# Eight experts on one core: x of four experts in one load, larger VectorE transposes, and evictions moved to ScalarE

## The chip, the cores and the metric

The kernel runs on one core of a Trainium2 chip. The metric is the device time of one execution in microseconds, as the median of several runs. Beside these runs there is one profiled execution, from which all views of the trace come.

## The reference

Eight experts each take their own 256 tokens through a two-layer network; nothing is routed.

```
x [8, 256, 512]   w1 [8, 512, 2048]   w2 [8, 2048, 512]   b1 [8, 2048]   b2 [8, 512]     all float32
h   = relu(x @ w1 + b1)        per expert: 256x512 times 512x2048
out = h @ w2 + b2              per expert: 256x2048 times 2048x512, float32
```

## The kernel before

**Stages.** For each expert e there are a load of `w1` (4 MB in DRAM), a load of `w2` (4 MB), transposes of x, a first product and a second product. The main loop has eleven steps s: it runs `first_product(s)` and, three steps behind (`LAG = 3`), `second_product(s - 3)`. Everything is computed in fp16 with fp32 accumulation; the DMAs that GpSimd issues cast fp32 to fp16 on the way, those that SyncE and ScalarE issue do not.

**Loads and their order.** All weight loads are issued by GpSimd, one after the other in an order written out by hand (the list `ring`), and they go through one software DMA queue. `w1` has three buffers, `w2` three. So the loads of w1 for experts 0, 1 and 2 are issued at once (`load_w1`, L84); the load of w1 for expert 3 has to wait until `first_product(0)` has read the first buffer, and what stands behind it in GpSimd's order (w2 of expert 0, x of experts 4 to 7) waits with it. The x of experts 0 and 1 comes as two SyncE loads of 512 KB (L190), 4 KB to a partition, in fp32, and VectorE casts each (L201). The x of experts 2 and 3 is one casting GpSimd load, that of experts 4 to 7 another (`load_x`, L76).

**Row order.** Where one load takes several experts, a partition holds several consecutive token rows, and the rows of one expert lie in P / n partitions. `transposes` turns x[token, hidden] into xT[hidden, token] by VectorE's 32x32 block transposes: L109 where an expert was loaded by itself (32x256 elements an instruction), L112 where two or four came together (32x256 and 32x512). They restore the plain column order with a strided write. ScalarE's relu with bias (L128) then writes `hT` in the order that the grouped stores want.

**First product.** 16 column blocks j of four matmuls (L121) into one of three PSUM tiles `ph`, each evicted by one relu on ScalarE, which needs the transposed bias `b1T` (VectorE, L208). In the middle of the loop (j = 8) the transposes of the next expert are emitted.

**Second product and stores.** For each half tb of the tokens a matmul with b2 (L171) and 16 matmuls (L178) into `po`. `store` evicts po[0] on VectorE (L156) and po[1] on ScalarE (L157); experts 0 to 3 are evicted in 4 pieces of 32 partitions a half, experts 4 and 5 in 2 pieces of 64, experts 6 and 7 in one. The results of experts 0 to 3 and of 4 and 5 are stored as two groups by GpSimd (`flush`, L140) after the last weight load; experts 6 and 7 are stored by SyncE and ScalarE (L164).

The instruction order within VectorE and ScalarE is set by a scheduler at build time, except for what `ordered` pins: the matmuls and GpSimd's DMAs.

Of the kernel before, what the change touches and what calls it, by code (L numbers as in the profile page):

```python
# [10 lines left out]
def kernel(  # L11
# [37 lines left out]
    w2_pool = ctx.enter_context(tc.tile_pool(name="w2", bufs=3))  # L49
    x_pool = ctx.enter_context(tc.tile_pool(name="xp", bufs=1))  # L50
# [18 lines left out]
    results = {}  # L69
    group_of = {first + i: (first, n) for first, n in GROUPS.items() for i in range(n)}  # L70

    def load_x(first, n):

        R = n * T // P
        t = x_pool.tile([P, R, H], fp16, tag=f"x{first}", name=f"x{first}")
        ordered(nc.gpsimd.dma_start(  # L76
            out=t, in_=x[first : first + n].rearrange("e (p r) h -> (e p) r h", r=R)
        ))
# [9 lines left out]
    def load_w2(e):  # L88
# [3 lines left out]
        for lo in range(0, nJ, half):  # L92
            ordered(nc.gpsimd.dma_start(out=w2_sb[e][:, lo : lo + half], in_=src[:, lo : lo + half]))  # L93

    def transposes(e):


        t, p0, R = x16[e]
        n = R // nTB
        xT[e] = xT_pool.tile([P, nKC, T], fp16, tag="xT", name="xT")  # L100
        for g in range(T // R // B):
            src = t[p0 + B * g : p0 + B * (g + 1)]
            for b in range(nB):
                block = src[:, :, b * (H // nB) : (b + 1) * (H // nB)].rearrange(
                    "p (n tb) (i kc) -> p tb kc n i", tb=nTB, kc=nKC)
                out = xT[e][b * B : (b + 1) * B].rearrange(
                    "p kc (tb g i n) -> p tb g kc n i", tb=nTB, i=B, n=n)
                if n == 1:
                    nc.vector.transpose(out=out[:, :, g, :, 0, :], in_=block[:, :, :, 0, :])  # L109
                    continue  # L110
                for tb in range(nTB):
                    nc.vector.transpose(out=out[:, tb, g], in_=block[:, tb])  # L112

    def first_product(e):
        hT[e] = hT_pool.tile([P, nJ, T], fp16, tag="hT", name="hT")
        split = group_of[e][1] if e in group_of else 1
        for j in range(nJ):
            bias_at = j * B + e * nB + nB - 1
            ph = psum_h.tile([P, T], fp32, tag="ph", name="ph")
            for kc in range(nKC):  # L120
                ordered(nc.tensor.matmul(  # L121
                    out=ph,
                    lhsT=w1_sb[e][:, kc, :].rearrange("p (q j) -> p q j", j=nJ)[:, :, j],
                    rhs=xT[e][:, kc, :],
                    start=(kc == 0),
                    stop=(kc == nKC - 1),
                ))
            nc.scalar.activation(  # L128
                out=hT[e][:, j, :].rearrange("p (tb k i) -> p tb k i", tb=nTB, k=split),
                in_=ph.rearrange("p (tb i k) -> p tb k i", tb=nTB, k=split),  # L130
                func=mybir.ActivationFunctionType.Relu,
                bias=b1T[:, bias_at : bias_at + 1],
                scale=1.0,
            )
            if j == nJ // 2 and e + 1 < E:
                transposes(e + 1)
# [5 lines left out]
    def store(e, po):  # L142
# [10 lines left out]
        at = (e - first) * rows  # L153
        for k in range(split):
            part = slice(k * rows, (k + 1) * rows)
            nc.vector.tensor_copy(out=out_sb[at : at + rows, k * nTB, :], in_=po[0][part])  # L156
            nc.scalar.copy(out=out_sb[at : at + rows, k * nTB + 1, :], in_=po[1][part])  # L157
        dst = out[first : first + n].rearrange("e (p r) h -> (e p) r h", r=split * nTB)
        if e in group_of:
            if e == first + n - 1:  # L160
# [23 lines left out]
                    ))  # L184
        store(e, po)

    x32 = []
    for e in range(nXF32):
        x32.append(out_pool.tile([P, nTB, H], fp32, tag="out", name="x32"))
        nc.sync.dma_start(out=x32[e], in_=x[e].rearrange("(p tb) h -> p tb h", tb=nTB))  # L190
    load_w1(0)
    ordered(nc.gpsimd.dma_start(  # L192
        out=b2_sb,
        in_=b2.rearrange("e h -> (e h)").rearrange("(o f) -> o f", o=1),
    ))
    ordered(nc.gpsimd.dma_start(out=b1_rows, in_=b1.rearrange("e (b i) -> (e b) i", b=nB)))  # L196
    nc.vector.memset(ones1, 1.0)  # L197

    for e in range(nXF32):
        t = x_pool.tile([P, nTB, H], fp16, tag=f"x{e}", name=f"x{e}")  # L200
        nc.vector.tensor_copy(out=t, in_=x32[e])  # L201
        x16[e] = (t, 0, nTB)
        if e == 0:
            transposes(e)


    for b in range(nB):
        nc.vector.transpose(  # L208
# [57 lines left out]
```

## Time and profile before

| | |
|---|---|
| median of 3 runs | 181.56 us (181.4 to 181.62) |
| span of the profiled execution | 179.8 us |
| median less span | 1.8 us, outside the profiled span |
| TensorE matmul busy | 129.0 us (72%) |
| VectorE busy | 87.8 us (49%) |
| ScalarE busy | 70.2 us (39%) |
| DMA | busy share 9 or more tenths in 38 of 40 slices |
| HBM read, written | 71.39 MB, 4.19 MB |

In the profile PE is TensorE's matmul, PEld its weight load, DVE is VectorE, ACT is ScalarE, POOL is GpSimd and SP is SyncE. The trailing q on an engine's name means its sequencer, which issues DMAs and handles semaphores. `x32` in the code is the fp32 staging tile of x; the trace names the loaded and the cast tile both `x`.

### The profile page before, as it was taken

What the parts mean: (1) busy time and instruction counts of PE and PEld (TensorE: products, weight loads), DVE (VectorE), ACT (ScalarE), POOL (GpSimd) and SP (SyncE); (2) the same over time, 40 slices, a digit from 0 to 9 for tenths busy, and PEclk for the clock granted to TensorE, in tenths of its full rate; (3) what the DMA queues carried; (4) which work ended last, traced back from release to release, by engine and by line L of the source; (5) the groups of instructions that cost most, each with busy time, mean ns of one, the idle gap of its engine ahead of it and who ended that gap; (6) DMA issues with size and microseconds to landing.
All of it is one profiled execution on the core that took longest, in us unless ns stands there. A gap on an engine that the chain in (4) does not pass through costs nothing.

```text
span 179.8 us, 1957 instructions
## 1 busy us (share of the span) xinstructions
PE 129.0 (72%) x784; PEld 86.2 (48%) x784; DVE 87.8 (49%) x125; ACT 70.2 (39%) x151; POOL 13.4 (7%) x28
## 2 busy tenths in 40 slices
PE   0005199959995930999869597969788887999740
PEld 0004089948993410794369244943387433343310
DVE  1999933985000199999999998000600020301010
ACT  0000569947993050482189005940298020111010
POOL 7000003020201010001000001000100020020000
PEclk9999999987999995599999799996999999999995
DMA  5999999999999999999999999999999999999995
GB/s 215 252 230 195 233 208 201 233 228 200 215 231 193 219 230 222 197 226 230 208 204 230 219 200 226 230 211 200 230 219 201 226 211 208 217 211 221 324 456 215
DMA packets 3828, 40.56 MB, mean 226 GB/s; under 512 B 460, under 2 KB 476, under 8 KB 1132
## 3 DMA queue, kind: packets, MB, share of 16 engines
q0 software_dynamic: 3232, 38.35, 96.5%
q1 hardware_dynamic: 476, 1.70, 2.4%
q10 hardware_dynamic: 112, 0.39, 0.5%
q8 instruction: 6, 0.10, 0.2%
q14 instruction: 2, 0.02, 0.0%
HBM read 71.39 MB, written 4.19 MB: 420 GB/s over the span
## 4 chain that ended last, share of the span: by engine, by line
DMA 55%; PE 32%; ACT 3%; another core or an unknown queue 3%; POOL 2%; issue 1%; POOLq 0%; ACTq 0%
DMA w1sb<-in_w_dram 43%; PE po L178 16%; PE ph L121 15%; DMA w2sb<-in_w_dram 12%; ACT out L157 3%; PE po L171 1%; POOL w1sb L84 1%; ACT hT L128 1%; POOL w2sb L93 0%; POOL x L76 0%; POOL b_sb L192 0%; POOL b_rows L196 0%; POOLq L250 0%; ACTq L128 0%
## 5 line engine op out<-in xcount | busy, mean ns | idle before, releaser
L121 PE MATMUL ph<-xT,w1sb 128*128 128x256 f16 x512 | 64.9, 293 | 34.1 <-DMA w1sb<-in_w_dram 21.5
L121 PEld LDWEIGHTS <-w1sb 128*128 128x128 f16 x512 | 59.8, 147 | 40.1 <-DMA w1sb<-in_w_dram 31.8
L178 PE MATMUL po<-w2sb,hT 128*128 128x512 f16 x256 | 60.0, 394 | 9.8 <-DMA w2sb<-in_w_dram 9.8
L112 DVE STREAM_TRANSPOSE xT<-x 32x256 f16<-32x256 f16 (+1 forms) x64 | 53.0, 888 | 26.0 <-DMA x<-in_x_dram 19.2
L128 ACT ACTIVATE hT<-ph,b1T 128x256 f16<-128x256 f32 x128 | 56.2, 474 | 14.4 <-PE ph L121 14.2
L178 PEld LDWEIGHTS <-hT 128*128 128x128 f16 x256 | 25.5, 101 | 44.1 <-issue 17.8
L156 DVE COPY out<-po 32x512 f32<-32x512 f32 (+2 forms) x22 | 15.1, 688 | 53.7 <-PE po L178 53.5
L157 ACT COPY out<-po 32x512 f32<-32x512 f32 (+2 forms) x22 | 12.7, 579 | 68.8 <-PE po L178 68.6
L109 DVE STREAM_TRANSPOSE xT<-x 32x256 f16<-32x256 f16 x32 | 14.0, 436 | 0.5
L93 POOL DMA_DIRECT2D w2sb<-in_w_dram x10 | 5.3, 534 | 71.6 <-PE po L178 71.6
L84 POOL DMA_DIRECT2D w1sb<-in_w_dram x8 | 4.8, 601 | 64.1 <-PE ph L121 63.3
L128 ACT ACT_TABLE_LOAD x1 | 1.3, 1283 | 20.1 <-DVE b1T L208 20.1
L171 PE MATMUL po<-b_sb,ones 1*128 1x512 f16 x16 | 4.8, 379 | 0.0
L208 DVE STREAM_TRANSPOSE b1T<-b_rows 32x512 f32<-32x512 f32 x4 | 4.1, 1031 | 0.1
L201 DVE CAST x<-x 128x1024 f16<-128x1024 f32 x2 | 1.4, 694 | 3.1 <-DMA x<-in_x_dram 3.1
L171 PEld LDWEIGHTS <-ones 1*128 1x128 f16 x16 | 0.9, 92 | 2.1 <-issue 2.1
L140 POOL DMA_DIRECT2D out_dram<-out x2 | 1.1, 538 | 9.8 <-ACT out L157 9.8
L76 POOL DMA_DIRECT2D x<-in_x_dram x2 | 1.1, 552 | 0.0
L197 DVE MEMSET ones<- 1x128 f16 x1 | 0.2, 165 | 0.8 <-PEq L250 0.8
L196 POOL DMA_DIRECT2D b_rows<-in_b_dram x1 | 0.5, 515 | 0.0
L192 POOL DMA_DIRECT2D b_sb<-in_b_dram x1 | 0.5, 513 | 0.0
L250 POOL MEMSET const-float32-0.0<- 128x1 f32 x1 | 0.1, 99 | 0.2 <-issue 0.2
(3 smaller groups left out, 0.3 us busy)
## 6 DMA issues: line engine op xcount, KB each, us to landing
w1sb<-in_w_dram POOLq DMA_DIRECT2D x8, 2048.0 KB, 34.8
w2sb<-in_w_dram POOLq DMA_DIRECT2D x6, 2048.0 KB, 47.2
w2sb<-in_w_dram POOLq DMA_DIRECT2D x4, 1024.0 KB, 23.2
out_dram<-out POOLq DMA_DIRECT2D x1, 2048.0 KB, 19.0
x<-in_x_dram SPq DMA_DIRECT2D x2, 512.0 KB, 3.7
x<-in_x_dram POOLq DMA_DIRECT2D x1, 1024.0 KB, 31.2
out_dram<-out POOLq DMA_DIRECT2D x1, 1024.0 KB, 14.9
x<-in_x_dram POOLq DMA_DIRECT2D x1, 512.0 KB, 24.0
```

The costliest lines, as they stand in the source:

```text
L84: ordered(nc.gpsimd.dma_start(out=w1_sb[e], in_=w1[e].rearrange("(p kc) m -> p kc m", kc=nKC)))
L93: ordered(nc.gpsimd.dma_start(out=w2_sb[e][:, lo : lo + half], in_=src[:, lo : lo + half]))
L109: nc.vector.transpose(out=out[:, :, g, :, 0, :], in_=block[:, :, :, 0, :])
L112: nc.vector.transpose(out=out[:, tb, g], in_=block[:, tb])
L121: ordered(nc.tensor.matmul(out=ph, lhsT=w1_sb[e][:, kc, :].rearrange("p (q j) -> p q j", j=nJ)[:, :, j], rhs=xT[e][:, kc, :], start=(kc == 0),
L128: nc.scalar.activation(out=hT[e][:, j, :].rearrange("p (tb k i) -> p tb k i", tb=nTB, k=split), in_=ph.rearrange("p (tb i k) -> p tb k i", ...
L156: nc.vector.tensor_copy(out=out_sb[at : at + rows, k * nTB, :], in_=po[0][part])
L157: nc.scalar.copy(out=out_sb[at : at + rows, k * nTB + 1, :], in_=po[1][part])
L171: ordered(nc.tensor.matmul(out=t, lhsT=ones1, rhs=b2_sb[0:1, e * H : (e + 1) * H], start=True, stop=False,))
L178: ordered(nc.tensor.matmul(out=po[tb], lhsT=hT[e][:, j, tb * P : (tb + 1) * P], rhs=w2_sb[e][:, j, :], start=False, stop=(j == nJ - 1),))
L201: nc.vector.tensor_copy(out=t, in_=x32[e])
L208: nc.vector.transpose(out=b1T[b * B : (b + 1) * B, nB - 1 - b : nB - 1 - b + nJ * B], in_=b1_rows.rearrange("r (i j) -> r j i", j=nJ),)
```

## The change

- The x of experts 0 to 3 comes in one SyncE load of 2 MB with 16 KB to a partition, into a tile that takes one of the three `w2` buffers; one VectorE cast of 128x4096 elements follows. The GpSimd load of x for experts 2 and 3 is gone; that for experts 4 to 7 stays.
- A partition now always holds 8 rows of one expert (32 partitions to an expert). `transposes` issues 4 instructions of 32x1024 elements for an expert, or, for experts 4 and 5, 8 of 32x512. The output columns are left in the row order of the load; only experts 6 and 7 get their order put right, by the relu's access pattern.
- `store` evicts both halves of experts 0 to 5 on ScalarE; for experts 6 and 7 it stays as it was.
- The memset of `ones1` moves from VectorE to GpSimd.

```diff
-    nXF32 = 2
-    X_LOADS = {2: 2, 4: 4}
+    XG = P // B
+    R = XG * T // P
+    ON_VECTOR = HALVED
...
-    def load_x(first, n):
-        R = n * T // P
+    def rows_of(first):
+        return x[first : first + XG].rearrange("e (p r) h -> (e p) r h", r=R)
+
+    def x_tile(first):
         t = x_pool.tile([P, R, H], fp16, tag=f"x{first}", name=f"x{first}")
...
-        for i in range(n):
-            x16[first + i] = (t, i * (P // n), R)
+        for i in range(XG):
+            x16[first + i] = t[i * B : (i + 1) * B]
+        return t
+
+    def load_x(first):
+        ordered(nc.gpsimd.dma_start(out=x_tile(first), in_=rows_of(first)))
...
+        s = 2 if split_of(e) == 2 else 1
         xT[e] = xT_pool.tile([P, nKC, T], fp16, tag="xT", name="xT")
+        for b in range(nB):
+            src = x16[e][:, :, b * (H // nB) : (b + 1) * (H // nB)].rearrange(
+                "p (s r) (i kc) -> p s kc r i", s=s, kc=nKC)
+            out = xT[e][b * B : (b + 1) * B].rearrange("p kc (r i s) -> p s kc r i", i=B, s=s)
+            for k in range(s):
+                nc.vector.transpose(out=out[:, k], in_=src[:, k])
...
+            columns = ph
+            hidden = hT[e][:, j, :]
+            if split_of(e) == 1:
+                columns = ph.rearrange("p (n tb i) -> p tb i n", tb=nTB, i=B)
+                hidden = hidden.rearrange("p (tb i n) -> p tb i n", tb=nTB, i=B)
             nc.scalar.activation(
-                out=hT[e][:, j, :].rearrange("p (tb k i) -> p tb k i", tb=nTB, k=split),
-                in_=ph.rearrange("p (tb i k) -> p tb k i", tb=nTB, k=split),
+                out=hidden,
+                in_=columns,
...
-            nc.vector.tensor_copy(out=out_sb[at : at + rows, k * nTB, :], in_=po[0][part])
-            nc.scalar.copy(out=out_sb[at : at + rows, k * nTB + 1, :], in_=po[1][part])
+            for tb in range(nTB):
+                to = out_sb[at : at + rows, tb * split + k, :]
+                if tb == 0 and e in ON_VECTOR:
+                    nc.vector.tensor_copy(out=to, in_=po[tb][part])
+                else:
+                    nc.scalar.copy(out=to, in_=po[tb][part])
...
-    x32 = []
-    for e in range(nXF32):
-        x32.append(out_pool.tile([P, nTB, H], fp32, tag="out", name="x32"))
-        nc.sync.dma_start(out=x32[e], in_=x[e].rearrange("(p tb) h -> p tb h", tb=nTB))
+    x32 = w2_pool.tile([P, R, H], fp32, tag="w2", name="x32")
+    nc.sync.dma_start(out=x32, in_=rows_of(0))
     load_w1(0)
...
-    nc.vector.memset(ones1, 1.0)
-
-    for e in range(nXF32):
-        t = x_pool.tile([P, nTB, H], fp16, tag=f"x{e}", name=f"x{e}")
-        nc.vector.tensor_copy(out=t, in_=x32[e])
-        x16[e] = (t, 0, nTB)
-        if e == 0:
-            transposes(e)
+    nc.gpsimd.memset(ones1, 1.0)
+
+    nc.vector.tensor_copy(out=x_tile(0), in_=x32)
+    transposes(0)
...
-            if s in X_LOADS:
-                ring.append((s - 2, load_x, (s, X_LOADS[s])))
+            if s % XG == 0:
+                ring.append((s - 2, load_x, (s,)))
```

More of the change, by code (lines that the diff above doesn't have):

```diff
@@ L70 @@
     group_of = {first + i: (first, n) for first, n in GROUPS.items() for i in range(n)}
-    def load_x(first, n):
-        R = n * T // P
+    def rows_of(first):
+        return x[first : first + XG].rearrange("e (p r) h -> (e p) r h", r=R)
+    def x_tile(first):
         t = x_pool.tile([P, R, H], fp16, tag=f"x{first}", name=f"x{first}")
-        ordered(nc.gpsimd.dma_start(
-            out=t, in_=x[first : first + n].rearrange("e (p r) h -> (e p) r h", r=R)
-        ))
-        for i in range(n):
-            x16[first + i] = (t, i * (P // n), R)
+        for i in range(XG):
[3 more added lines that the diff above has]
+        ordered(nc.gpsimd.dma_start(out=x_tile(first), in_=rows_of(first)))
     def load_w1(e):
@@ L93, in load_w2, with split_of @@
             ordered(nc.gpsimd.dma_start(out=w2_sb[e][:, lo : lo + half], in_=src[:, lo : lo + half]))
+    def split_of(e):
+        return group_of[e][1] if e in group_of else 1
     def transposes(e):
-        t, p0, R = x16[e]
-        n = R // nTB
+        s = 2 if split_of(e) == 2 else 1
         xT[e] = xT_pool.tile([P, nKC, T], fp16, tag="xT", name="xT")
[L101 to L112, printed above, removed]
+        for b in range(nB):
[4 more added lines that the diff above has]
+                nc.vector.transpose(out=out[:, k], in_=src[:, k])
     def first_product(e):
         hT[e] = hT_pool.tile([P, nJ, T], fp16, tag="hT", name="hT")
-        split = group_of[e][1] if e in group_of else 1
         for j in range(nJ):
```

## The prediction

> **What bounds the kernel now.** I read the page's slices and queues first, because a kernel that reads 71 MB in 180 us is likely to be held by its loads.
>
> ```profile
> span 179.8 us, 1957 instructions
> PE   0005199959995930999869597969788887999740
> DVE  1999933985000199999999998000600020301010
> DMA  5999999999999999999999999999999999999995
> GB/s 215 252 230 195 233 208 201 233 228 200 215 231 193 219 230 222 197 226 230 208 204 230 219 200 226 230 211 200 230 219 201 226 211 208 217 211 221 324 456 215
> q0 software_dynamic: 3232, 38.35, 96.5%
> q1 hardware_dynamic: 476, 1.70, 2.4%
> HBM read 71.39 MB, written 4.19 MB: 420 GB/s over the span
> ```
>
> The DMA row is full in every slice but the first and the last, while PE has holes of whole slices. GB/s counts bytes as they are written, so a casting load shows at half of what it reads. The two HBM figures add to 75.6 MB. So the end is set by how soon the DMA engines start, by their rate, and by whether they ever run dry. Next I asked how far ahead of need each load is issued: the timeline of GpSimd and SyncE, and the issue-to-landing time of single loads. First the timeline:
>
> ```profile
> 0.74 0.87 SPq L190 DMA_DIRECT2D x<-in_x_dram  x2
> 1.25 0.67 POOL L84 DMA_DIRECT2D w1sb<-in_w_dram  x1 [0.80 <-POOLq L250]
> 4.00 0.91 POOL L84 DMA_DIRECT2D w1sb<-in_w_dram  x1
> 29.93 0.53 POOL L84 DMA_DIRECT2D w1sb<-in_w_dram  x1 [25.03 <-PE ph L121]
> 30.45 0.54 POOL L93 DMA_DIRECT2D w2sb<-in_w_dram  x1
> 109.72 2.34 ACT L157 COPY out<-po 32x512 f32<-32x512 f32 x4 [10.61 <-PE po L178]
> 147.22 1.06 POOL L93 DMA_DIRECT2D w2sb<-in_w_dram  x2 [16.62 <-PE po L178]
> 158.11 1.07 POOL L140 DMA_DIRECT2D out_dram<-out  x2 [9.83 <-ACT out L157]
> 164.81 0.38 ACTq L164 DMA_DIRECT2D out_dram<-out  x1
> ```
>
> Then, from the view of a line, the landing times of the loads issued at 1.25, 4.00, 29.93 and 30.45 (w1 of experts 0, 2 and 3, w2 of expert 0) and of the two at 147.22 (w2 of expert 7), in this order:
>
> ```profile
> DMA to landing us min/median/max: 14.0/14.0/14.0
> DMA to landing us min/median/max: 34.6/34.6/34.6
> DMA to landing us min/median/max: 17.7/17.7/17.7
> DMA to landing us min/median/max: 26.8/26.8/26.8
> DMA to landing us min/median/max: 16.9/19.3/21.6
> ```
>
> w1 of expert 3 lands at 29.9 + 17.7 = 47.6 and the w2 behind it at 30.5 + 26.8 = 57.3: one 4 MB load takes 9.7 us of the DMA engines, 433 GB/s read. The last weights were issued at 147.2 and landed up to 21.6 us later, though the two halves need only 9.7: there the queue is some 12 us ahead. At one place it is thinner. All that GpSimd could issue at the start is landed at 4.0 + 34.6 = 38.6, and the next load waits until 29.93 for PE to finish the first product of expert 0. Its transfer fills 37.9 to 47.6, so it had 8.0 us in hand, less the time from issue to the first byte. That time is at most about 3.4 us (next fence: the software queue moves nothing before 4.6, issued at 1.25) and at least about 1 us (SyncE issues at 0.74, and the first slice of the window from 1.5 with data starts at 1.73). **So the first product of expert 0 may end about 4.6 to 7 us later than now, at 34.5 to 37, before the DMA engines run dry.** This is the number on which the sign hangs.
>
> **The load of x.** The bytes in 40 slices and the queues of the window from 1.5 to 4.6 us, and the queue of weights in that from 4.6 to 14.2:
>
> ```profile
> GB/s 0 0 0 211 0 0 0 0 264 159 476 317 529 317 529 317 476 370 476 370 423 370 476 370 370 476 317 476 317 529 317 529 317 529 317 529 264 581 264 581
> q1 hardware_dynamic: 265, 1.02, 85.3%
> q0 software_dynamic: 128, 2.10, 102.9%
> ```
>
> Until 4.6 only SyncE's 1 MB moves (hardware queue), then w1 of expert 0. The removed load of experts 2 and 3 lies in the software queue between w1 of experts 1 and 2. The same 2 MB of DRAM are read either way, only 1 MB of it earlier: w1 of expert 0 comes 2.4 us later (1.05 MB at 433 GB/s) and w1 of expert 2 when it did before. In rate, 1.02 MB took about 2.9 us in the first window (1.73 to 4.6), 0.4 of it ramp, so 2.5 against 2.42 at the weights' rate: rows of 16 KB can gain some 0.1 us on each MB that used to come in other rows, 0.0 to 0.25 us in all. I take 0.15 us gained.
>
> **The chain to the first product's end**, which must fit into those 4.6 to 7 us. Its rows:
>
> ```profile
> 4.09 0.69 DVE L201 CAST x<-x 128x1024 f16<-128x1024 f32 x1 [3.10 <-DMA x<-in_x_dram]
> 4.82 7.18 DVE L109 STREAM_TRANSPOSE xT<-x 32x256 f16<-32x256 f16 x16
> 12.76 3.13 DVE L109 STREAM_TRANSPOSE xT<-x 32x256 f16<-32x256 f16 x7
> 15.90 4.17 DVE L208 STREAM_TRANSPOSE b1T<-b_rows 32x512 f32<-32x512 f32 x4
> 20.14 1.28 ACT L128 ACT_TABLE_LOAD   x1 [20.14 <-DVE b1T L208]
> b_rows<-in_b_dram POOLq DMA_DIRECT2D x1, 64.0 KB, 13.2
> L112 DVE STREAM_TRANSPOSE xT<-x 32x512 f16<-32x512 f16 x32 | 40.3, 1331 | 19.8 <-DMA x<-in_x_dram 19.2 <-PE ph L121 0.3
> L109 DVE STREAM_TRANSPOSE xT<-x 32x256 f16<-32x256 f16 x32 | 14.0, 436 | 0.5
> L112 DVE STREAM_TRANSPOSE xT<-x 32x256 f16<-32x256 f16 x32 | 12.7, 444 | 6.2 <-PE ph L121 6.0
> ```
>
> 1. Landing: 512 KB were ready for VectorE at 4.09. Another 1.57 MB at 412 to 433 GB/s (the rates of the last paragraph) add 3.6 to 3.8: 7.8.
> 2. Cast: 4 times the elements, at most 4 x 0.694 = 2.8; a fixed part that is paid once lowers it. I take 2.6: 10.4.
> 3. Transposes of expert 0: no row has 32x1024. Per element the rows give 436/256 = 1.70 ns (one expert a load), 1.73 (two) and 1331/512 = 2.60 (four). The instruction's length isn't what makes the dear row dear, I think, but its write: with n experts a load the inner output step is n elements, 1, 2 and 4. The new code writes expert 0 with inner step 1, like L109. So 4 x 1024 x 1.70 = 7.0, a little less for fewer starts: 6.9, with 10.6 (at 2.60) as the dear end and 6.4 as the cheap one. End: 17.3.
> 4. Bias: `b1_rows` landed at 2.41 + 13.2 = 15.6 behind w1 of expert 0, and now comes 2.4 later, 18.0. VectorE may by then be in a transpose of expert 1 (1.7 long; now the scheduler puts 7 of 16 ahead of the bias). I take 18.9; 4.17 of work: 23.1.
> 5. From the bias's end (20.07) to the first product's end (29.93) it took 9.86 us, with the table load and 52 matmuls in it. Unchanged: 32.9.
>
> That is 3.0 us later than now, inside the 4.6 to 7. No hole, and nothing later is late: the second product that frees w2's first reused buffer is the same (x takes one of three buffers, read out by 10.4, so the fourth w2 load still waits for the second product of expert 0).
>
> **The other parts** are off the path. Evictions: 20 of 22 VectorE copies go to ScalarE, where one takes 2.34/4 = 0.585 us, 11.7 us more of ScalarE's 179.8. If they run in loop order, 7 instead of 4 stand between PE's end of a second product and the next relu, 1.75 us for each of experts 0 to 3, 0.6 for 4 and 5; if the scheduler puts the first half's four ahead, nothing. The relus and so PE's next first product wait behind them. The cover is the queue's lead, 12 us at the last weight load, 11 at the grouped stores, issued at 158.11 behind weights that land at 147.7 + 21.6 = 169.3; without it each would count in full. VectorE's transposes for experts 4 to 7 fall from 32 x 1.331 = 42.6 to about 4 x 7 = 28 us, which helps nobody while DMA is full. ScalarE's relus keep their element count; their new access pattern could cost or save a little of 0.47 us each, under the same cover. The memset on GpSimd is 0.1 us, before or behind issues that are ahead. The last store starts when the DMA engines have worked off what is queued, so it moves with the sum.
>
> **The sum:** 179.8 - 0.15 = 179.65 of span, and with the 1.8 us outside it (181.56 - 179.8) 181.4 us. A measurement of this kernel can tell about 0.2%, 0.36 us, from no change, so this is "the same".
>
> **The rivals.** *A: the weight queue runs dry once, at about 36 us, because x comes late (slower).* SyncE's load and w1 of expert 0 may share the engines. For it, a window with both kinds of queue busy (168.6 to 170.6):
>
> ```profile
> q0 software_dynamic: 68, 0.52, 62.0%
> q10 hardware_dynamic: 63, 0.26, 31.4%
> q1 hardware_dynamic: 21, 0.08, 9.5%
> ```
>
> 68 packets of one against 84 of the others: they alternate. Against it, the row of 164.9 to 168.2:
>
> ```profile
> q0 software_dynamic: 104, 0.77, 105.5%
> ```
>
> The stores issued at 164.81 got nothing for over 3 us: what an engine already has goes first, and at the start SyncE's rows are there first. If they alternate from 4.6 on, 16 KB of x against 32 KB of w1, the x left by then (about 1 MB) takes 3.15 MB at 433 GB/s, 7.3 us: ready at 12.3 instead of 7.8. Then step 3 ends at 21.8, the bias at 26.0, the first product at 35.9: against 34.5 to 37 that is a hole of 0 to 1.4 us, up to 182.8. With the dear transposes instead (x at 7.8, 10.6 for step 3) the first product ends at 35.1 and the hole is 0 to 0.6; with both, or with several of expert 1's transposes ahead of the bias as well, 39 to 41 and 2 to 6 us, 183.5 to 187. It decides from an end of the first product of about 35 us. Chance 0.26, 182.8 the nearest price.
>
> The Trainium skill, DMA: Bandwidth & Descriptors, section Queues, rings and completion order, says that a DMA engine goes round-robin between the queue rows it has work for, packet by packet. By that rule x shares from the moment w1's packets exist, which is the case just priced; the trace bears it out late (168.6) but not for the first 3 us of a newcomer.
>
> *B: the rows of 16 KB move as pieces of 4 KB (the load is not what its words say).* The hardware queue shows only 4 KB rows so far (1.02 MB in 265 packets, some of them tiny). In alternation with packets of w1 that read 32 KB, 1 MB of x would be held back behind 8 MB of weights, to about 4.6 + 9.4/0.433 = 26 us, and by steps 2 to 5 the first product ends near 50: a hole of 13 to 15 us, 195 or so. Against it, those 4 KB are whole contiguous rows, not cut ones. Chance 0.06.
>
> *C: faster by more than 0.36 us.* If the DMA engines have losses that I don't see, around the software load of x between two weight loads or from VectorE's strided writes, they go. Against it: slices with VectorE idle (11 to 13: 215, 231, 193) and busy (15 to 17: 230, 222, 197) show the same GB/s. It would give about 180.9. Chance 0.12.
>
> **The numbers.** Forecast 0.56. Faster is C, 0.12; slower is B and A with 0.06 and 0.26; the same is the forecast, 0.56. The range runs from C's 181.0 over the forecast and A's single causes to 184.0; outside lie B, A's combinations and the better half of C. The forecast's own range is 181.2 to 181.7.
>
> **What would show it.** Right: the DMA row full from the second slice on; the hardware queue alone until about 7; the cast at 7.8; four transposes of about 1.7 us; the GpSimd issue that waits for PE (now 29.93) at 32 to 34; span 179.5 to 179.9. Wrong: a gap in the DMA row near 36 to 40 us (A), a cast after 12 (A) or after 20 (B), transposes of 2.6 us each (A's other cause), a weight load's 9.7 us changed (C).

## The result, and the profile after

The changed kernel takes 182.41 us (median of 6 runs, 182.28 to 183.41) against 181.56 us before. The ratio is 1.0061, with a 95% interval of 1.0043 to 1.0079: slower by 0.85 us, where 181.4 and no change had been forecast. 0.6 us of it lie in the span (median 180.4 over the six runs, against 179.8), 0.28 outside it (the six runs lie 2.08 above their spans on average; before it was 1.80).

The page of the profile after, the lines that answer to those of before:

```profile
span 180.3 us, 1896 instructions
DVE  0009996468200099307300910000000000001010
DMA  5999999999999999999999999999999999999995
GB/s 174 320 262 245 204 207 233 225 200 211 229 220 194 227 229 204 214 225 218 200 222 233 211 207 222 225 204 214 229 218 200 222 214 209 214 214 216 335 442 218
q0 software_dynamic: 3088, 37.82, 94.6%
q1 hardware_dynamic: 332, 2.75, 4.1%
HBM read 71.39 MB, written 4.19 MB: 419 GB/s over the span
```

The DMA row is as full as before, and the bytes are the same, so no slice-wide gap opened. VectorE is nearly idle from the middle on, and nobody gained by it. The first slice moved less: 174 GB/s against 215. The timeline of the first 35 us of the kernel after (start, length, engine, line, operation; in brackets the idle time before it and what ended it):

```profile
0.75 0.39 SPq L195 DMA_DIRECT2D x<-in_x_dram  x1
13.48 2.29 DVE L204 CAST x<-x 128x4096 f16<-128x4096 f32 x1 [13.48 <-DMA x<-in_x_dram]
15.80 4.98 DVE L111 STREAM_TRANSPOSE xT<-x 32x1024 f16<-32x1024 f16 x4
20.82 4.18 DVE L208 STREAM_TRANSPOSE b1T<-b_rows 32x512 f32<-32x512 f32 x4
34.48 0.53 POOL L87 DMA_DIRECT2D w1sb<-in_w_dram  x1 [30.31 <-PE ph L119]
```

x lands at 13.48 and not at 7.8; the cast and the transposes are shorter than reckoned; the first product still ends at 34.2, and the issue that waits for it stands at 34.48, at the very start of the 34.5 to 37 that the prediction gave as the edge, the latest end of that product before the weight queue runs dry. Why x is late shows in the queues between 6 and 12 us (packets, MB, share of 16 engines' time):

```profile
q0 software_dynamic: 55, 0.90, 70.2%
q1 hardware_dynamic: 48, 0.79, 31.2%
```

55 packets of weights stand beside 48 of x: the two queues alternate. x moves in packets of 16 KB (0.79 MB in 48), and one takes 0.312 x 96 / 48 = 0.62 us. The Trainium skill, DMA: Bandwidth & Descriptors, section Queues, rings and completion order, has the DMA engines go round-robin between their queues by packets; here that holds from the first weight packet on.

Where the span's 0.5 us is lost shows in the landings of the weights. First the time from issue to landing of the load of w1 for expert 3, the first that waits for PE, here for the kernel after.

```profile
DMA to landing us min/median/max: 13.8/13.8/13.8
```

It lands at 34.48 + 13.8 = 48.3; before it was 29.93 + 17.7 = 47.6. From there to the end of the span are 132.0 and 132.2 us. In 18 of the 20 profiled kernels and executions told of here this rest is 131.6 to 132.4 (the other two are `pad` and `dense2`). So what the change does to the span, it has done by 48 us, as far as this range of 0.8 us tells, and before the first eviction that it moves (the first copy of L164 starts at 61.6). Much of it is done earlier still, well ahead of the edge: w1 of expert 1, issued at 2.91 before and at 3.05 after, takes to its landing, before and then after:

```profile
DMA to landing us min/median/max: 22.1/22.1/22.1
```

```profile
DMA to landing us min/median/max: 25.1/25.1/25.1
```

It lands at 25.0 and at 28.2, 3.2 us apart, and the 1.05 MB of x that now go ahead of it account for 2.4 of them. One execution is coarse at this size: in `evict_alone` below, whose x is loaded as before, w1 of expert 3 lands at 48.2 too, yet the span is 179.9. These rows point at the start; the medians of the experiments have to decide. In the first microseconds there is this, from 2 to 4 us (columns: length, busy time and count of PE, PEld, DVE, ACT, POOL, granted clock, DMA share, GB/s), first of the kernel before, then after:

```profile
2.00:4.00 2.00, 0.00 (x0) 0.00 (x0) 0.00 (x0) 0.00 (x0) 2.00 (x4) 1.00 0.92 371
```

```profile
2.00:4.00 2.00, 0.00 (x0) 0.00 (x0) 0.00 (x0) 0.00 (x0) 2.00 (x5) 1.00 0.75 238
```

0.27 MB fewer in these 2 us, which is 0.6 us of the later 433 GB/s, with only x in flight in both. A packet of 16 KB takes longer here than the 0.62 us above: in the window from 1.5 to 4.6 of the kernel after,

```profile
q1 hardware_dynamic: 53, 0.87, 89.8%
```

53 packets share 0.898 x 16 x 3.1 = 44.5 us, 0.84 us each. In the same window SyncE's queue had moved 1.02 MB before; the 0.15 MB between are 0.35 us. (`evict_alone`, with x as before, moved 0.88 MB there at no cost in time, so this window by itself proves little.) w1 of expert 0, next in line, lands at 1.25 + 17.2 = 18.5 after 15.3 before (the prediction allowed for 2.4 of these 3.2).

For the part outside the span, the row of the instruction queue in the window from 181 to 183 us of the kernel after, which lies behind the span's end:

```profile
q14 instruction: 1, 0.01, 1.1%
```

Both kernels have two such packets. One stands near 50 us in both; the other came at 37.9 before, in the midst of the work, and comes at 182.2 after. VectorE's program fell from 125 to 47 instructions.

The remaining rows, groups by line and form of the kernel after (busy us, mean ns of one, idle time before):

```profile
L111 DVE STREAM_TRANSPOSE xT<-x 32x1024 f16<-32x1024 f16 x24 | 29.7, 1236 | 26.9 <-PE ph L119 26.6
L111 DVE STREAM_TRANSPOSE xT<-x 32x512 f16<-32x512 f16 x16 | 10.8, 717 | 16.8 <-DMA x<-in_x_dram 16.7
L164 ACT COPY out<-po 32x512 f32<-32x512 f32 x32 | 18.4, 576 | 26.2 <-PE po L185 26.0
```

### The profile page after: what moved, and what is told of

The parts are those of the page before. It is cut to its first block, busy times and chain, and to the rows that moved or that the text cites. A ratio compares the mean times of both kernels' runs of the same rounds, so it can differ in the third digit from the quotient of the medians.

```text
span 180.3 us, 1896 instructions
## 1 busy us (share of the span) xinstructions
PE 125.1 (69%) x784; PEld 84.7 (47%) x784; DVE 48.2 (27%) x47; ACT 81.6 (45%) x171; POOL 12.6 (7%) x28
## 4 chain that ended last, share of the span: by engine, by line
DMA 63%; PE 18%; DVE 6%; issue 6%; ACT 1%; another core or an unknown queue 1%; POOL 0%; POOLq 0%; ACTq 0%
DMA w1sb<-in_w_dram 44%; PE ph L119 12%; DMA w2sb<-in_w_dram 12%; DMA x<-in_x_dram 7%; PE po L185 6%; DVE xT L111 3%; DVE b1T L208 2%; DVE x L204 1%; ACT L131 1%; ACT out L164 0%; PE po L178 0%; POOL w2sb L96 0%; ACT hT L131 0%; POOLq L87 0%
## 5 line engine op out<-in xcount | busy, mean ns | idle before, releaser
L119 PE MATMUL ph<-xT,w1sb 128*128 128x256 f16 x512 | 62.6, 287 | 38.0 <-DVE xT L111 20.8
L119 PEld LDWEIGHTS <-w1sb 128*128 128x128 f16 x512 | 58.8, 147 | 42.6 <-DMA w1sb<-in_w_dram 34.1
L185 PE MATMUL po<-w2sb,hT 128*128 128x512 f16 x256 | 58.4, 386 | 10.2 <-DMA w2sb<-in_w_dram 10.2
L111 DVE STREAM_TRANSPOSE xT<-x 32x1024 f16<-32x1024 f16 (+1 forms) x40 | 40.4, 1028 | 43.7 <-PE ph L119 26.6
L164 ACT COPY out<-po 32x512 f32<-32x512 f32 (+2 forms) x42 | 24.2, 577 | 56.0 <-PE po L185 55.7
L162 DVE COPY out<-po 128x512 f32<-128x512 f32 x2 | 1.4, 692 | 66.8 <-PE po L185 66.8
L204 DVE CAST x<-x 128x4096 f16<-128x4096 f32 x1 | 2.3, 2293 | 13.5 <-DMA x<-in_x_dram 13.5
L83 POOL DMA_DIRECT2D x<-in_x_dram x1 | 0.6, 557 | 0.0
```

Source lines behind the costliest of these rows:

```text
L111: nc.vector.transpose(out=out[:, k], in_=src[:, k])
L119: ordered(nc.tensor.matmul(out=ph, lhsT=w1_sb[e][:, kc, :].rearrange("p (q j) -> p q j", j=nJ)[:, :, j], rhs=xT[e][:, kc, :], start=(kc == 0),
L162: nc.vector.tensor_copy(out=to, in_=po[tb][part])
L164: nc.scalar.copy(out=to, in_=po[tb][part])
L185: ordered(nc.tensor.matmul(out=po[tb], lhsT=hT[e][:, j, tb * P : (tb + 1) * P], rhs=w2_sb[e][:, j, :], start=False, stop=(j == nJ - 1),))
L204: nc.vector.tensor_copy(out=x_tile(0), in_=x32)
```

## The experiments

The theory after this result had three parts: x starts slowly, the late x brings the weight queue near its edge, and something is added outside the span. The rivals were a loss through sharing, one through the evictions, and the size of the pieces of x.

### halves: x in two loads of 8 KB to a partition

```diff
-    nc.sync.dma_start(out=x32, in_=rows_of(0))
+    for lo in range(0, R, R // 2):
+        nc.sync.dma_start(out=x32[:, lo : lo + R // 2], in_=rows_of(0)[:, lo : lo + R // 2])
```

> The changed kernel with x of experts 0 to 3 in two SyncE loads of 8 KB pieces (4 of the 8 rows of each partition) instead of one of 16 KB pieces. Start-up theory: in the changed kernel the first packets of 16 KB take 1.1 to 1.7 us instead of 0.61 and all later loads land 0.5 us later than before; with 8 KB pieces the first packets are shorter and about half of that comes back: w1 of expert 2 landed about 0.25 us earlier, time about 182.1 us. If only the spacing of the rows in DRAM (16 KB from partition to partition) makes the start slow, nothing comes back: 182.4. Rival (alternation): 8 KB pieces alternate with packets of w1 that read 32 KB, so what is left of x at 5.7 us is held back twice as long, x lands after 17 us instead of 13.5, the first product of expert 0 ends after 38 and the weight queue runs dry for 1 to 3 us: 183.5 to 185.5.

186.37 us against 181.85, ratio 1.0244 (1.0222 to 1.0266), more than even the rival expected. The timeline, and the windows from 37 to 39:

```profile
17.68 2.29 DVE L205 CAST x<-x 128x4096 f16<-128x4096 f32 x1 [17.68 <-DMA x<-in_x_dram]
38.66 0.53 POOL L87 DMA_DIRECT2D w1sb<-in_w_dram  x1 [34.50 <-PE ph L119]
...
37.00:38.00 1.00, 1.00 (x12) 1.00 (x11) 0.00 (x0) 1.00 (x4) 0.00 (x0) 1.00 0.01 0
38.00:39.00 1.00, 1.00 (x12) 1.00 (x11) 0.60 (x1) 1.00 (x4) 0.34 (x1) 1.00 0.00 0
```

With half the bytes in a packet x gets half the share beside w1, lands 4.2 us later, and the hole of rival A is there: PE busy, DMA at nothing, 0 GB/s. The weight queue does run dry near 37, as the prediction's edge says, and whoever issues at 38.66 pays some 4 us. In the change the edge is held with little to spare. It also shows what 16 KB rows do for the change: rows of 8 KB come too late.

### pad: 96 small instructions more on VectorE

```diff
     nc.gpsimd.memset(ones1, 1.0)
+    pad = singles.tile([1, 32], fp32)
+    for _ in range(96):
+        nc.vector.memset(pad, 0.0)
```

> The changed kernel with 96 short VectorE memsets of a scratch tile added. Theory of the end: the changed kernel's time lies 2.0 us above its span, that of before 1.8, and in its trace a last 8 KB instruction packet stands at 182.2 us, behind the span, where before had one at 37.9; VectorE's program has become short enough that its last block is fetched only at the end. With 96 more instructions the fetch comes early again and the time outside the span goes back to 1.8: 182.2 us, same span. Rival: the fetch has nothing to do with it, or another engine makes it: 182.4 or slightly more.

182.9 us, ratio 1.0065 (1.0042 to 1.0088); spans 180.6 to 182.0. No instruction packet stands behind the span's end any more (the two come at 20.0 and 50.6 us), and the part outside the span falls from 2.08 to 1.95, half of what had been added. The span itself is no better, and in the profiled execution (span 181.2) the issue that waits for the first product stands at 35.37, 0.9 us later than in the change, and 0.5 us more are lost after 48.5 us, which stays unexplained. So `pad` alone proves little; `evict_back` is the cleaner test.

### b1first: the bias rows ahead of x on SyncE

```diff
+    nc.sync.dma_start(out=b1_rows, in_=b1.rearrange("e (b i) -> (e b) i", b=nB))
     nc.sync.dma_start(out=x32, in_=rows_of(0))
...
-    ordered(nc.gpsimd.dma_start(out=b1_rows, in_=b1.rearrange("e (b i) -> (e b) i", b=nB)))
```

> The changed kernel with b1 loaded by SyncE ahead of x instead of by GpSimd behind w1 of expert 0. The transposed bias is then ready long before x; the first product of expert 0 ends about 30 instead of 34.5 us. Theory of the edge: the two runs of six at 183.2 to 183.4 with spans of 181.1 to 181.3 come from a weight queue that runs dry by 1 us because the first product ends at 34.5, at the edge of its cover; they vanish here and the spread falls to 0.2 us. Theory of the start-up: a small load goes first, the first packets of x are no longer the first of all; if it is the coldness of the engines that makes them slow, x's packets are at 0.61 us and the time falls to about 182.0, else it stays at 182.3 to 182.4.

182.39 us against 181.85, ratio 1.0029 (1.0016 to 1.0043), spans 180.3 to 180.5. x starts 0.45 us later, yet the bias no longer stands in VectorE's way, and the waiting issue moves from 34.48 to 32.49 (about 30 had been expected). The kernel is steadier than the change and no faster in its best runs: its slowest run is 182.7 against 183.41 for the change, so distance from the edge takes the late runs away and leaves the rest of the loss.

### split64: x of experts 0 and 1 alone, in 64 partitions

```diff
-    nc.sync.dma_start(out=x32, in_=rows_of(0))
+    nc.sync.dma_start(out=x32[:64], in_=rows_of(0)[:64])
...
-    nc.vector.tensor_copy(out=x_tile(0), in_=x32)
+    nc.vector.tensor_copy(out=x16t[:64], in_=x32[:64])
...
+    ring.append((0, load_x23, ()))     # experts 2, 3 by GpSimd, ahead of w1 of expert 2
```

> The changed kernel with x of experts 0 and 1 (64 partitions of 16 KB, 1 MB) by SyncE and that of experts 2 and 3 by the casting GpSimd load where it was before the change: the division of bytes between the queues is that of before, the rows are still 16 KB. Start-up theory: the slow first packets of 16 KB are still there, so w1 of expert 2 still lands 0.4 to 0.5 us late and the time is 182.2 to 182.4; x lands by about 6 us and the first product of expert 0 ends below 31. Rival (it is the size of the SyncE load, 2 MB, or its alternation with w1 that loses): 181.6 to 181.8.

183.67 us, ratio 1.0098 (1.0083 to 1.0112); neither theory had it. The window from 3 to 4 us, and the cast:

```profile
3.00:4.00 1.00, 0.00 (x0) 0.00 (x0) 0.00 (x0) 0.00 (x0) 1.00 (x3) 1.00 1.22 262
...
8.20 2.28 DVE L205 CAST x<-x 64x4096 f16<-64x4096 f32 x1 [8.20 <-DMA x<-in_x_dram]
```

The load moves 262 GB/s in each microsecond from 2 to 6, a little over half of 433, where the change's load into 128 partitions reaches 426 from 4 on. The kernel thus has a slow start of another kind and could not answer its question. The Trainium skill, SBUF — State Buffer, section Door 1: The DMA port swizzle, says that partitions 0 to 63 reach only 8 of the 16 ports; the 262 GB/s agree in kind, though the page's asymptote for them, 218, is lower than what was measured.

### hold and hold_quarters: GpSimd's first load held back by 1.4 us

```diff
     nc.sync.dma_start(out=x32, in_=rows_of(0))
+    hold = singles.tile([P, 1024], fp32)
+    for _ in range(2):
+        ordered(nc.gpsimd.memset(hold, 0.0))
```

`hold_quarters` has the same and x in four loads of 4 KB to a partition.

> The changed kernel with GpSimd kept busy for about 2.1 us by two memsets of a scratch tile ahead of its first weight load, so that w1 of expert 0 joins the engines when x is nearly through. No alternation: x lands at about 8 instead of 13.5 and the first product of expert 0 ends near 31 instead of 34.5, 4 us ahead of the edge. Start-up theory: the first 16 KB packets are as slow as in the changed kernel, w1 of expert 2 lands within 0.2 us of where it did, spans of 180.2 to 180.5 in every run and none at 181 or more: 182.1 to 182.3 us. Rival (the alternation itself loses the 0.5 us, for instance through packets of 0.624 instead of 0.611): the weights land 0.4 us earlier and the time is 181.8.

> The same held-back weight load, and x in four SyncE loads of 4 KB pieces (2 of the 8 rows of each partition); the pieces are 16 KB apart in DRAM. Start-up theory by size: the first packets are as short as those of the kernel before and the loss is gone: weights land as in the kernel before within 0.1 us, 181.6 to 181.8. Start-up theory by spacing: 16 KB from partition to partition is what makes the first accesses slow, the loss stays: 182.1 to 182.3.

`hold` took 182.89 us, ratio 1.0056 (1.0038 to 1.0073), with spans from 179.8 to 181.2; `hold_quarters` 188.92, ratio 1.0388 (1.0364 to 1.0412). The casts and the waiting issue of `hold`, then the cast of `hold_quarters`:

```profile
12.28 2.29 DVE L207 CAST x<-x 128x4096 f16<-128x4096 f32 x1 [12.28 <-DMA x<-in_x_dram]
33.22 0.54 POOL L87 DMA_DIRECT2D w1sb<-in_w_dram  x1 [27.77 <-PE ph L119]
```

```profile
19.30 2.29 DVE L208 CAST x<-x 128x4096 f16<-128x4096 f32 x1 [19.30 <-DMA x<-in_x_dram]
```

A miss: x was to land near 8 in `hold` and landed at 12.28, only 1.2 us sooner; 1.4 us of a slow start move little. The waiting issue is 1.3 us further from the edge, and the span still varies as much as the change's. It misses at the fast end too: two of its ten runs (spans 179.8 and 179.9), and the first of two further executions told below (179.9), are as fast as the kernel before, with rows of x 16 KB apart. So the loss at the start doesn't always reach the end; why not is open. `hold_quarters` shows rival B's price in a mild form: with 4 KB packets x lands at 19.30 and the issue waits until 41.35. It also starts slowly (229 GB/s from 2 to 4 us) with 4 KB packets, which first spoke against the size of the packet as the cause.

### b1act: the bias rows on ScalarE's queue

```diff
     nc.sync.dma_start(out=x32, in_=rows_of(0))
+    nc.scalar.dma_start(out=b1_rows, in_=b1.rearrange("e (b i) -> (e b) i", b=nB))
...
-    ordered(nc.gpsimd.dma_start(out=b1_rows, in_=b1.rearrange("e (b i) -> (e b) i", b=nB)))
```

> The changed kernel with b1 loaded by ScalarE's queue at the start instead of by GpSimd behind w1 of expert 0; x is issued when it was. In the run with b1 ahead of x on SyncE, x began 0.45 us later and all weights landed 0.85 us later than before the change, 0.4 more than in the changed kernel. Edge theory: the first product of expert 0 ends 2 us earlier than in the changed kernel, no run at 183; start-up theory: the 0.5 us stay. 182.1 to 182.3, spread 0.3.

182.3 us, ratio 1.0032 (1.002 to 1.0044), every span 180.2 or 180.3. The waiting issue and its landing:

```profile
29.84 0.53 POOL L87 DMA_DIRECT2D w1sb<-in_w_dram  x1 [26.18 <-PE ph L119]
...
DMA to landing us min/median/max: 18.5/18.5/18.5
```

The issue is 4.6 us ahead of the change's, where it stood before the change, and the load lands at 29.84 + 18.5 = 48.3, as in the change's own profile. w1 of expert 1 lands alike in both, at 28.1 here and at 28.2 in the change. So in that profile the edge costs little if anything, and what is left, 0.3 to 0.4 us of span (180.2, against medians of 179.8 and 179.9 of the kernel before) and 2.07 outside it, comes from neither the edge nor the late first product.

### evict_back: VectorE has its 20 evictions back

```diff
-    ON_VECTOR = HALVED
+    ON_VECTOR = range(E)
```

> The changed kernel with the evictions of experts 0 to 5 divided between VectorE and ScalarE as before the change. All three theories (start-up, edge, end) leave the span as it is: 180.2 to 180.5, with some runs at 181, 182.3 to 182.6 us. Rival (ScalarE's 11.7 us of extra copies delay first products, later weight issues and the end): 181.8 to 182.0.

182.39 us, ratio 1.0042 (1.0029 to 1.0055). Outside the span there are 1.80 us, as in the kernel before, and the last instruction packet comes at 90.4 us; VectorE has 67 instructions. The span, 180.3 to 181.2, is no better; in the profiled execution the waiting issue stands at 35.17. So the 0.28 us outside go with the evictions that left VectorE, and the span's part doesn't.

### evict_alone: the kernel before, with the evictions of experts 0 to 5 on ScalarE

```diff
-            nc.vector.tensor_copy(out=out_sb[at : at + rows, k * nTB, :], in_=po[0][part])
+            (nc.vector.tensor_copy if e in HALVED else nc.scalar.copy)(
+                out=out_sb[at : at + rows, k * nTB, :], in_=po[0][part])
```

> The kernel before with the evictions of experts 0 to 5 on ScalarE and nothing else changed. VectorE keeps some 105 instructions here, the changed kernel has 47. In the changed kernel the time outside the span is 2.08 us, with the evictions put back 1.80, like before the change. Theory of the late fetch (a VectorE program too short to fetch its last block before the end): the fetch stays early here, outside 1.80, span as before, ratio 0.999 to 1.001. Rival (ScalarE's longer program or its copies cost it): outside 2.0 to 2.1, 0.2 to 0.3 us slower than before.

181.72 us against 181.63, ratio 1.0001 (0.9992 to 1.001). Moving the evictions costs nothing by itself, in the span or outside it (1.83): with VectorE at 105 instructions the two instruction packets come at 38.0 and 48.8, as before the change.

### spaced: the kernel before, its x rows 16 KB apart in DRAM

```diff
-        nc.sync.dma_start(out=x32[e], in_=x[e].rearrange("(p tb) h -> p tb h", tb=nTB))
+        nc.sync.dma_start(out=x32[e], in_=x[0:4].rearrange(
+            "e (p r) h -> (e p) r h", r=8)[:, 2 * e : 2 * e + 2])
```

> The kernel before with nothing changed but the rows that its two SyncE loads read: the same 4 KB pieces in the same number and order, but 16 KB apart in DRAM instead of next to each other (so experts 0 and 1 compute on other tokens of experts 0 to 3). Start-up theory by spacing: the engines move 0.25 MB less in the first 5 us, as in the changed kernel; all weights land 0.4 to 0.6 us later than in the kernel before, 182.1 to 182.3 us. Start-up theory by size of the piece: as before, within 0.15 us.

182.07 us against 181.63, ratio 1.0022 (1.0013 to 1.0031), every span 180.2 or 180.3. The window from 2 to 4 us:

```profile
2.00:4.00 2.00, 0.00 (x0) 0.00 (x0) 0.00 (x0) 0.00 (x0) 2.00 (x5) 1.00 0.87 233
```

The same number and size of pieces as before, the same instructions on every engine; only which rows are read differs (so experts 0 and 1 get other tokens, and only the time counts). The kernel has the change's slow start and loses 0.44 us. Its waiting issue stands at 31.04, far from the edge, and its w1 of expert 1 lands at 25.9, 0.9 us later than before. The size of the piece isn't the cause. Nor is sharing: up to 4.6 us x is alone in both kernels, and 0.74 MB have moved instead of 1.02. The spacing of the rows of x by itself costs as much as was left of the span's loss in `b1act`.

### b1act_evict: `b1act` and `evict_back` together

> The changed kernel with b1 on ScalarE's queue and the evictions divided as before: the edge and the late fetch are both gone and only the start-up loss is left. If the parts add: span 180.2 as with b1 on ScalarE's queue alone, 1.80 outside, 182.0 us, spread 0.2; 0.3 to 0.4 slower than before.

182.1 us, ratio 1.0026 (1.0016 to 1.0036), spans 180.2 to 180.4, 1.79 outside. Away from the edge and with the late fetch gone, what is left is 0.47 us, the same as in `spaced`. The parts add.

### two_queues: the kernel before, x of expert 1 on ScalarE's queue

```diff
-        nc.sync.dma_start(out=x32[e], in_=x[e].rearrange("(p tb) h -> p tb h", tb=nTB))
+        (nc.sync if e == 0 else nc.scalar).dma_start(out=x32[e], in_=x[e].rearrange("(p tb) h -> p tb h", tb=nTB))
```

> The kernel before with x of expert 1 loaded by ScalarE's queue instead of SyncE's. If the start of the kernel before is itself held by how fast one queue hands out its first pieces, the engines fill sooner and everything comes 0.1 to 0.2 us earlier, 181.4 to 181.5; if it is the DRAM's first accesses, nothing changes (within 0.1 us), or the two loads' rows 512 KB apart disturb each other and it is 0.1 to 0.3 slower.

181.61 us against 181.63, ratio 0.9995 (0.9985 to 1.0006): a second queue doesn't change the time, though from 2 to 4 us this profile shows 305 GB/s instead of 371.

### after_look1, after_look2, hold_look1, hold_look2: two more executions each of the change and of `hold`

> The changed kernel once more, for one more profile. Two of its six runs had spans of 181.1 and 181.3, the others 180.1 to 180.4. Edge theory: in a profile with a span over 180.8 the GpSimd issue that waits for the first product of expert 0 stands after 34.9 us, and the load of w1 of expert 3 ends more than 9.7 us after that of expert 2, by the excess of the span; in one with a span of 180.4 or less it stands before 34.9. Rival (the start itself varies): the weights of expert 2 land later by the excess, and the issue stands where it was.

> The same kernel and the same two readings as in the look before it.

> The kernel with the first weight load held back once more, whose spans ran from 179.8 to 181.2 although its first product of expert 0 ended at 33.2 in the one profile. Edge theory: in a run over 180.7 x lands a turn or two later than 12.3, the waiting issue stands after 34.9 and the queue shows the hole. Rival (the start varies): w1 of expert 2 lands up to 1 us later without a hole.

> The same kernel and the same two readings as in the look before it.

The change took 182.22 (span 180.2) and 182.89 (span 180.7). The waiting issue, its landing and the windows from 30 to 32 of `after_look1`, then of `after_look2`:

```profile
34.42 0.54 POOL L87 DMA_DIRECT2D w1sb<-in_w_dram  x1 [30.25 <-PE ph L119]
...
DMA to landing us min/median/max: 13.6/13.6/13.6
...
30.00:31.00 1.00, 1.00 (x11) 1.00 (x10) 0.00 (x0) 0.77 (x2) 0.00 (x0) 1.00 0.54 115
31.00:32.00 1.00, 1.00 (x12) 1.00 (x11) 0.00 (x0) 1.00 (x4) 0.00 (x0) 1.00 0.92 197
```

```profile
35.43 0.53 POOL L87 DMA_DIRECT2D w1sb<-in_w_dram  x1 [31.27 <-PE ph L119]
...
DMA to landing us min/median/max: 13.1/13.1/13.1
...
30.00:31.00 1.00, 1.00 (x7) 0.77 (x6) 0.02 (x1) 0.61 (x2) 0.00 (x0) 1.00 0.92 197
31.00:32.00 1.00, 1.00 (x7) 0.81 (x6) 0.00 (x0) 0.47 (x1) 0.00 (x0) 1.00 0.61 131
```

In the second execution PE has 7 matmuls in each of these microseconds where the first has 11 and 12, at a granted clock of 1.00 in both; the first product ends 1.0 us later, and w1 of expert 3 lands at 48.5 instead of 48.0, the 0.5 us by which the spans differ. The load takes 13.1 us from its issue. Where the queue certainly was dry it took 13.1 (`hold_quarters`) and 13.7 (`halves`), so here it had next to nothing queued ahead of it. The 13.6 of the first execution and the 13.8 of the change's own profile are no longer than that: these issues stand at the edge itself, and a microsecond later is paid in part. `evict_back` (issue at 35.17, 13.2) and `pad` (35.37, 13.1) stand beyond it, by the same reading.

`hold` took 182.11 (span 179.9) and 182.88 (span 180.7). The second, with its issue at 33.97:

```profile
33.97 0.53 POOL L87 DMA_DIRECT2D w1sb<-in_w_dram  x1 [28.51 <-PE ph L119]
...
DMA to landing us min/median/max: 14.6/14.6/14.6
```

This doesn't fit. It issues earlier than the change and lands at 48.6, against 33.27 + 14.4 = 47.7 in the first. Some 0.9 us were lost ahead of that landing while the issue was 0.5 us inside the edge. So the edge accounts for the change's late runs as far as these two executions go, but not for `hold`'s spread.

### spaced32 and dense2: the kernel before, with other rows of x

```diff
+        nc.sync.dma_start(out=x32[e], in_=x.rearrange(
+            "e (p r) h -> (e p) r h", r=16)[:, 2 * e : 2 * e + 2])
```

```diff
+        nc.sync.dma_start(out=x32[e], in_=x[e].rearrange("(tb p) h -> p tb h", tb=nTB))
```

> As the run with the rows 16 KB apart, but 32 KB: the kernel before, its two SyncE loads reading the same 4 KB pieces in the same number from all eight experts' x (experts 0 and 1 compute on other tokens). If the spacing in DRAM sets the loss at the start, it is at least as large as with 16 KB, 0.45 us or more: 182.1 to 182.5. If only the move away from contiguous rows counts, the same 182.07 as with 16 KB.

> The other direction: the kernel before, its two SyncE loads reading pieces of 2 KB that lie next to each other from partition to partition (token t of expert 0 and 1 goes to partition t mod 128, so these experts' rows come out in another order). Theory by spacing, carried on: a spacing of 2 KB starts no slower than one of 4 KB, and if the kernel before still loses something at its start (it has moved 1.14 MB by 5 us, 0.26 less than 433 GB/s from 1.77 on would), part of it comes back: 181.3 to 181.6. Rival: pieces of 2 KB cost more packets and it is 0.1 to 0.3 us slower.

`spaced32` (pieces of 4 KB, 32 KB apart): 181.61 us against 181.58, ratio 1.0003 (0.9994 to 1.0012). `dense2` (pieces of 2 KB side by side): 181.97, ratio 1.0017 (1.0002 to 1.0032), spans 179.9 to 181.2. From 2 to 4 us, first `spaced32`, then `dense2`:

```profile
2.00:4.00 2.00, 0.00 (x0) 0.00 (x0) 0.00 (x0) 0.00 (x0) 2.00 (x5) 1.00 0.81 313
```

```profile
2.00:4.00 2.00, 0.00 (x0) 0.00 (x0) 0.00 (x0) 0.00 (x0) 2.00 (x4) 1.00 0.97 369
```

Twice the spacing costs nothing, so "the further apart, the slower" is wrong; 16 KB is worse than either 4 KB or 32 KB. `dense2` starts as fast as the kernel before, and in its profile (span 181.2) w1 of expert 3 lands at 47.9, so it loses its time later than the start; where was not pursued.

## Why the prediction was wrong, step by step

**The load of x: the step that failed.** "I take 0.15 us gained" was wrong in sign. The rows of the window before, 4 KB pieces side by side at 0.4 us of ramp and then nearly the weights' rate, were carried over to rows of 16 KB, on the reasoning that larger rows can only gain. They start more slowly: `spaced` has that loss without anything else of the change, 0.44 us, and `b1act_evict` leaves 0.47 as the one remainder. The term should have been about 0.45 us lost, with a range to both sides. The trace of before had no row of x with that spacing, so nothing in it bore out a bound of 0 to 0.25 us that left no room for a loss. That the 0.45 us in the change are the same loss as in `spaced` is argued from the like size and the like slow start; in three executions of `hold` it doesn't show.

**The 1.8 us outside the span.** They were added as a constant. They are 2.08 after. All seven kernels with 47 instructions on VectorE show an instruction packet 1.6 to 2.0 us behind the span's end, and have 1.99 to 2.34 us outside it on average; the seven changed ones with 67 to 125 instructions have none there and 1.78 to 1.83; `pad`, with 143, has none and 1.95. `evict_back` shows that the 0.28 us go when VectorE gets its 20 evictions back. That the length of its program counts, and that the fetch is what takes the time, is argued: `pad` has the longest program and got only half of it back.

**The chain, step by step.** Landing: 13.48 instead of 7.8, wrong by 5.7 us; rival A's mechanism (x and w1 alternate) was the true one, and its own 12.3 was 1.2 short, in part through the slow start. Cast: 2.29 for 2.6. Transposes: 4.98 us for 6.9, since one took 1.236 us, 1.21 ns an element, below the cheapest row of before (1.70). So the length does count: 436 ns for 32x256 and 1236 for 32x1024, both with step 1, make some 0.17 us an instruction and 1.04 ns an element (an estimate from these two rows). That the strided write was the dear part fits, 717 ns with an output step of 2 elements against 1331 with 4, at 32x512. Bias: it followed at once, 20.82 to 25.0, with no transpose of expert 1 between. From the bias's end to the waiting issue, which the prediction took for the end of the product: 9.48 for 9.86. Together the errors, +5.7, -0.3, -1.9, -1.6 (the wait ahead of the bias) and -0.4, give 34.4 for 32.9; measured 34.48. That no hole opened in the profiled execution was luck: the errors cancel. Two sums of the prediction are slightly off without deciding anything: 1.02 MB at 433 GB/s take 2.36 us, not 2.42, and 4.6 + 7.3 is 11.9, where rival A has 12.3.

**The edge and rival A.** "34.5 to 37" fits: issues at 34.48 and 34.42 show no hole, those at 38.66 and 41.35 one of whole microseconds. A's time of 182.8 was near, but its hole is no part of the profiled execution; two of the six runs (spans 181.3 and 181.1) and `after_look2` have more than the rest. Sum of the medians: 0.45 for the start, 0.1 to 0.2 for the edge (180.4 against `b1act`'s 180.2 to 180.3; argued, not shown), 0.28 outside, together 0.83 to 0.93 for the measured 0.85.

**Rival B** was wrong: the rows of 16 KB move whole, 0.87 MB in 53 packets. **Rival C** found nothing: GB/s are the same with VectorE idle.

**The other parts** held: the 32x512 copies take 0.576 us (0.585 reckoned), and `evict_alone` is at 1.0001.

**Open:** why rows 16 KB apart start slowly and those 32 KB apart don't. The Trainium skill, DMA: Bandwidth & Descriptors, section Latency and other measured facts, tells of copies slowed by rows 512 KiB and more apart and infers that partitions in step then use the same memory channels; no run here shows whether that is at work at 16 KB. Open too are the spread of `hold` and `dense2`, and why `hold` is at times as fast as the kernel before. No version here beats the kernel before.

## What to carry to other kernels

Where loads fill the whole span, the end moves with the landing of the first load that has to wait for an engine: read that time first, and subtract. A load that is moved to the very start should be priced by a row of the same rows of memory, since the first microseconds are not the steady state, and without such a row its bound should reach to both signs. What lies outside the span is a term of the sum like any other and can change with the program.

## What the runs showed of the hardware that was not expected

- The first load of an execution depends on which rows it reads: 1 MB of x in pieces of 4 KB cost the kernel 0.44 us more with the pieces 16 KB apart than side by side, and nothing more with 32 KB. From 2 to 4 us they moved 233, 371 and 313 GB/s. These rates are coarse: with the load of x untouched it was 293 in `evict_alone`, at no cost in time.
- An instruction packet came 1.9 us after the span's end, once VectorE's program was short (47 instructions), and the time outside the span grew by 0.28 us.
- Two queues share by packets, not by bytes: beside packets of w1, the 2 MB of x landed at 13.48 in packets of 16 KB, at 17.68 in packets of 8 KB. From 8 to 12 us 32 packets of x stand beside 34 of w1 in the first case, 48 beside 43 in the second.
- From 30 to 32 us, within the first product, PE had 7 matmuls a microsecond in one execution and 11 to 12 in another, at the same granted clock of 1.00 in the records.
